# A planner of on-chip buffers: a half buffer passes over a just-freed half when more than three slots are free, not more than seven

## The chip, the cores and the metric

The kernel runs on one core of a Trainium2 chip. The metric is the device time of one execution in microseconds. "Before" is the kernel as it was, "after" the kernel with the change. A step is one count of the kernel's `self.i`, mostly one product of 24 matmuls.

## The reference

One inference step of a small decoder of two layers, a pooling mixer (layer A) and an attention mixer (layer B), for 1024 prompt tokens and 8 sample tokens, model width 2048, all in float32.

```python
def pool_layer(x, prefix, pos, w_in, w_grp, scale, w_out, g_ln, b_ln):
    z = x @ w_in                                   # 2048 x 4096
    u, gate = z[..., :D_POOL], z[..., D_POOL:]
    d, new_state = multiscale_pool(u, prefix, pos) # trailing means over 2, 4, 8, 16
    d = einsum('btgc,gce->btge', d in 4 groups, w_grp) * scale
    y = (d * silu(gate)) @ w_out
    return layer_norm(ALPHA * x + y, g_ln, b_ln), new_state

def attn_layer(x, pos, kb, vb, ..., w_in, sinks, w_out, g_ln, b_ln):
    z = x @ w_in                                   # queries and gate
    q = rope_partial(z[..., :D_ATTN], pos)
    o = attn_core(q, kb, vb, q_pos, k_pos, sinks)  # window of 128, 4 KV heads, a sink per head
    y = (o * silu(gate)) @ w_out
    return layer_norm(ALPHA * x + y, g_ln, b_ln)
```

Between the two, keys and values are projected once (`w_kv`). The outputs are both token sets and the new pooling states, keys and values.

## The kernel before

The tokens are cut into two chunks: chunk 0 has 512 prompt tokens, chunk 1 the other 512 and the 8 sample tokens. The work runs in phases: `ai` (the input projection of layer A) for chunk 0 and 1, `ao` (its output projection), `bi` (keys, values, queries, gates and attention of layer B) and `bo` (its output projection). The names below carry the chunk: `bi1`, `bo0`.

Nearly all products are done by a Strassen-like scheme (`seven`): seven products of 1024 x 128 weights with half a chunk of tokens instead of eight, their results added and subtracted by ScalarE (ACT) and VectorE (DVE) while TensorE (PE) goes on. float32 values are split into a high and a low part of the type fp32r (`cast_to` by ACT, L508; `prep_to` by DVE, L523), and each product takes three matmuls for each of eight blocks (L687, L688, L689): 24 matmuls. The sums of weight blocks that the scheme needs are made on DVE (L352 in `first_pair`, `sum_gen` at L460 and above) and stored to DRAM by POOL for the other chunk.

The order of the work is fixed when the program is built. PE, DVE and ACT each carry out their instructions in the order of the source (`in_order`); SP issues nearly all loads and POOL nearly all stores, each in its own order. What falls to one step is settled by the planner: `begin` loads, casts and prepares weights some products ahead, `end` runs what was put down for the step (`product`, `at`), the token blocks of the next phase (`x_tick`) and side work (`sum_gen`, `t_gen`, `ln_gen`). Several of these ask how many slots are whole: `begin` looks less far ahead with under three (`bi1`) or five (`bo0`) whole slots, `sum_gen` of `wob` starts a load only with more than five, `x_tick` and the side work have bounds of their own.

All working buffers come from one pool, `Mem`: 54 slots, each of two halves. `full` takes the whole free slot that was given back longest ago. `half` takes the free half of a slot whose other half is in use ("part-free"), the one given back longest ago, or else half of a whole free slot. Time is counted by `clock`, one tick for each buffer given back. A buffer that a store still reads is given back with `free(True)` and counts as ten ticks younger. Who writes a buffer next must wait until its last readers are done: the planner's choice decides whom a writer waits for.

Lines that matter below:

- L626 to L658: the steps of `seven`. `p2` (L631, L632) takes a half, `o["s"]`, and ACT copies a PSUM bank into it; `p4` (L653) is DVE's last reading, after which it is freed. L635, L641, L647, L660 are ACT's other copies out of a bank.
- L925 to L939: `j_steps`, the sum of a pair of rows for a mean: `add` takes a half and DVE writes the sum (L929), ACT casts it (L935), DVE takes the rest (L939) and frees the half. `j_sum` is the matmul behind it (L955).
- L1374: `shifted` puts these three at steps n, n+1, n+2 in `bo0` for its first pair; L1344 is the residual sum ahead of it, L1383 and L1387 use the mean.
- L1753 to L1770: `rope` takes a half that a load fills (L1755), and gives it back to a store.
- L1961, L1962, L1977: the softmax weights leave PSUM (ACT, DVE), and PE multiplies them with the values.
- L1984 to L1989: `gate` takes a half, DVE writes the attention's result (L1986), POOL stores it (`o<-m`, L1989), and the half is given back with `free(True)`.
- L2040: `decode`, the attention of the sample tokens, a chain of ten short steps through all engines: L2096 to L2098 are DVE's part of the softmax, L2102 PE's transpose behind it, L2105 the copy of that. Its second half runs at the start of `bo0`.

Of the kernel before, what the change touches and what calls it, by code (L numbers as in the profile page):

```python
# [139 lines left out]
class Mem:  # L140
# [22 lines left out]
    def half(self, n=TMAX):  # L163
        fits = lambda i: i < NWIDE or n <= 512
        part = [
            (a if b is None else b, i) for i, (a, b) in enumerate(self.f) if (a is None) != (b is None) and fits(i)
        ]
        if part and min(part)[0] > self.clock - 6 and len(self.whole()) > 7:
            part = []
        i = min(part)[1] if part else min((i for i in self.whole() if fits(i)), key=lambda i: max(self.f[i]))  # L170
        h = 0 if self.f[i][0] is not None else 1
        if not part:
            self.new(i)
        self.f[i][h] = None
        w = TMAX if i < NWIDE else 512
        return Slot(self, i, h, self.t[i][:, h * w : (h + 1) * w])
# [2332 lines left out]
```

## Time and profile before

| | |
|---|---|
| median of 3 runs | 2312.7 us (2311.48 to 2317.13) |
| profiled execution | 2315.52 us, its span 2313.7 us |
| PE busy | 2285.5 us, 99% of the span |
| DVE, ACT, POOL busy | 1904.7, 1388.2, 218.4 us |
| mean granted clock of PE | 0.997 |
| DMA | 647.77 MB, mean 280 GB/s |

How to read it. The busy time of PE is the union of its matmuls, which overlap: one lasts some 282 ns, and the next starts long before its end. A wait is put down as "who, line <- whom it waited for"; in a row of the time order the wait stands in brackets behind the instruction that waited. The span's time axis places the phases: `bi0` begins at about 1075 us, `bi1` at about 1500, `bo0` at about 1940, `bo1` at about 2125.

### The profile page before, as it was taken

Reading aid. Unit: us, or ns where it says so; the run is one execution under the profiler, and the core shown is the slowest. Engines: PE = TensorE matmul, PEld = TensorE weight load, DVE = VectorE, ACT = ScalarE, POOL = GpSimd, SP = SyncE. Lnnn points to the kernel's source line nnn. Section 1 sums busy time; section 2 is a strip of 40 time slices with the busy share of each in tenths; the row PEclk is TensorE's granted clock in tenths of the full one; section 3 lists DMA queues with packets and bytes.
Section 4 is the critical chain, followed back from the end, with each engine's and each line's share of the span. In section 5 each row is a group of like instructions: output and inputs, shape, how many; then the busy total and the mean of one; then the engine's idle time right before and its main releaser. Section 6 shows DMA issues by size and latency. Waiting matters only on the chain. (4 is left out here: it accounts for less than half of the span.)

```text
span 2313.7 us, 50523 instructions
## 1 busy us (share of the span) xinstructions
PE 2285.5 (99%) x20353; PEld 2214.5 (96%) x20353; DVE 1904.7 (82%) x2413; ACT 1388.2 (60%) x2551; POOL 218.4 (9%) x399
## 2 busy tenths in 40 slices
PE   9999999999999999999999999999999999899998
PEld 8999999999999999999889999999999999899998
DVE  8888889877878878988868888899776777788997
ACT  5544446444546556555567676785676678556665
POOL 0111110010000000000111111100010100010001
PEclk9999999999999999999999999999999999999999
DMA  7779679988889989999777767777776779699894
GB/s 259 266 263 316 228 249 330 314 305 301 301 305 322 338 286 331 320 385 343 236 249 238 243 225 251 268 264 234 242 247 224 250 238 315 210 359 363 297 333 150
DMA packets 252028, 647.77 MB, mean 280 GB/s; under 512 B 27504, under 2 KB 112528, under 8 KB 251792
## 3 DMA queue, kind: packets, MB, share of 16 engines
q1 hardware_dynamic: 208640, 490.20, 63.2%
q0 software_dynamic: 43152, 154.34, 17.3%
q8 instruction: 159, 2.61, 0.5%
q14 instruction: 77, 0.63, 0.1%
HBM read 467.21 MB, written 177.23 MB: 279 GB/s over the span
## 5 line engine op out<-in xcount | busy, mean ns | idle before, releaser
L687 PE MATMUL pD<-m,m 128*128 128x260 f32 (+1 forms) x5088 | 1443.6, 284 | 4.9 <-ACT pD L626 2.2
L689 PE MATMUL pD<-m,m 128*128 128x260 f32 (+1 forms) x5088 | 1436.2, 282 | 6.0 <-DVE m L523 5.7
L688 PE MATMUL pD<-m,m 128*128 128x260 f32 (+1 forms) x5088 | 1436.5, 282 | 0.0
L687 PEld LDWEIGHTS pD<-m,m 128*128 128x128 f32 x5088 | 960.7, 189 | 14.8 <-issue 7.2
L689 PEld LDWEIGHTS pD<-m,m 128*128 128x128 f32 x5088 | 961.4, 189 | 8.0 <-DVE m L523 8.0
L688 PEld LDWEIGHTS pD<-m,m 128*128 128x128 f32 x5088 | 960.8, 189 | 0.5
L523 DVE TENSOR_TENSOR m<-m,m 128x1024 fp32r<-128x1024 f32 x690 | 833.4, 1218 | 94.6 <-ACT m L508 32.2
L508 ACT CAST m<-m 128x1024 fp32r<-128x1024 f32 x690 | 720.6, 1049 | 231.6 <-DVE m L352 118.5
L352 DVE TENSOR_TENSOR m<-m,m 128x1024 f32<-128x1024 f32 x136 | 166.2, 1222 | 15.1 <-DMA m<-in_wia 10.4
L850 DVE TENSOR_TENSOR m<-m,m 128x1024 fp32r<-128x1024 f32 (+1 forms) x118 | 144.0, 1225 | 4.4 <-ACT m L841 3.8
L841 ACT CAST m<-m 128x1024 fp32r<-128x1024 f32 (+1 forms) x118 | 123.4, 1053 | 4.5 <-DMA m<-in_x 2.4
L648 DVE TENSOR_TENSOR m<-pD,m 128x260 f32<-128x260 f32 (+1 forms) x92 | 39.0, 424 | 101.4 <-ACT pD L647 95.3
L660 ACT COPY m<-pD 128x260 f32<-128x260 f32 (+1 forms) x88 | 32.8, 372 | 122.4 <-PE pD L689 121.8
L1935 ACT ACTIVATE m<-m,sm 128x128 f32<-128x128 f32 x256 | 99.3, 392 | 0.0
L632 ACT COPY m<-pD 128x260 f32<-128x260 f32 (+1 forms) x90 | 33.6, 373 | 97.8 <-PE pD L689 93.1
L1184 PE MATMUL pD<-m,m 128*128 128x260 f32 (+1 forms) x528 | 91.5, 323 | 0.0
L715 PE MATMUL pD<-m,m 128*128 128x512 f32 x224 | 89.0, 397 | 0.0
L635 ACT COPY m<-pD 128x260 f32<-128x260 f32 (+1 forms) x92 | 34.4, 374 | 90.8 <-PE pD L689 90.7
L717 PE MATMUL pD<-m,m 128*128 128x512 f32 x224 | 88.2, 394 | 0.0
L716 PE MATMUL pD<-m,m 128*128 128x512 f32 x224 | 88.2, 394 | 0.0
L1184 PEld LDWEIGHTS pD<-m,m 128*128 128x128 f32 x528 | 79.4, 188 | 8.2
L1948 ACT ACTIVATE m<-m,sm 128x128 f32<-128x128 f32 x256 | 81.9, 393 | 2.7 <-DVE sm L1943 2.5
(259 smaller groups left out, 2082.4 us busy)
## 6 DMA issues: line engine op xcount, KB each, us to landing
m<-in_wib SPq DMA_DIRECT2D x132, 512.0 KB
m<-in_wia SPq DMA_DIRECT2D x128, 512.0 KB
m<-swoa SPq DMA_DIRECT2D x64, 512.0 KB
swia<-m POOLq DMA_DIRECT2D x56, 512.0 KB, 4.6
m<-swia SPq DMA_DIRECT2D x56, 512.0 KB
m<-swob SPq DMA_DIRECT2D x56, 512.0 KB
m<-in_wob SPq DMA_DIRECT2D x52, 512.0 KB
m<-in_woa SPq DMA_DIRECT2D x48, 512.0 KB
```

What stands on the lines that cost most here:

```text
L352: self.nc.vector.tensor_add(s[out].a[:, :1024], s[x].a[:, :1024], s[y].a[:, :1024])
L508: self.nc.scalar.copy(hi.r[:, :1024], self.stream[self.cast].src().a[:, :1024])
L523: self.nc.vector.tensor_sub(lo.r[:, :1024], s.src().a[:, :1024], hi.a[:, :1024])
L687: nc.tensor.matmul(ps[:, :TH], wh[:, s], h, start=new and k == 0, stop=False, skip_group_check=on)
L688: nc.tensor.matmul(ps[:, :TH], wh[:, s], l, start=False, stop=False, skip_group_check=on)
L689: nc.tensor.matmul(ps[:, :TH], wl[:, s], h, start=False, stop=k == 7, skip_group_check=on)
L715: nc.tensor.matmul(ps[:], wh[:, s], h, start=par == 0 and k == 0, stop=False)
L716: nc.tensor.matmul(ps[:], wh[:, s], l, start=False, stop=False)
L841: self.nc.scalar.copy(h.r[:, :n], s.a[:, :n])
L850: self.nc.vector.tensor_sub(l.r[:, :n], s.a[:, :n], h.a[:, :n])
L1184: nc.tensor.matmul(ps[:, : cs.stop - cs.start], ws[:, s], d[:, cs], start=f0 and k == 0, stop=l0 and k == 3,)
L1935: nc.scalar.activation(x["s3"][:, i, :], x["s3"][:, i, :], AF.Exp, bias=nm[:, i : i + 1], scale=0.125, accum_out=rs[:, i : i + 1],)
```

## The change

In `Mem.half`, a part-free half that was given back within the last six ticks is passed over, and a whole free slot is opened instead, when more than three slots are whole. Before, that took more than seven. Everything else is the same code.

```diff
-        if part and min(part)[0] > self.clock - 6 and len(self.whole()) > 7:
+        if part and min(part)[0] > self.clock - 6 and len(self.whole()) > 3:
             part = []
```

The slots of all later buffers can differ from the first request on at which the two conditions differ, and with them the number of whole slots that the planner's other bounds read.

## The prediction

> **What bounds the kernel now.** I read the page's head first, then the busy time by stretch, then who waited for whom in the stretch where TensorE lost most, then DVE, PE and POOL in order of time there.
>
> ```profile
> span 2313.7 us, 50523 instructions
> PE 2285.5 (99%) x20353; PEld 2214.5 (96%) x20353; DVE 1904.7 (82%) x2413; ACT 1388.2 (60%) x2551; POOL 218.4 (9%) x399
> ```
> ```profile
> core 0: us, PE busy (x) PEld busy (x) DVE busy (x) ACT busy (x) POOL busy (x), PEclk, DMA share, GB/s
> 700.00:900.00 200.00, 200.00 (x1689) 199.92 (x1688) 160.03 (x185) 114.76 (x162) 10.72 (x18) 1.00 0.90 312
> 1232.00:1500.00 268.00, 267.86 (x2988) 261.43 (x2987) 230.18 (x279) 186.15 (x445) 43.80 (x84) 1.00 0.71 244
> 1560.00:1990.00 430.00, 428.45 (x4719) 417.96 (x4719) 322.11 (x444) 295.36 (x690) 37.00 (x58) 1.00 0.75 246
> 1990.00:2060.00 70.00, 63.33 (x549) 62.17 (x548) 58.05 (x74) 35.05 (x58) 8.01 (x15) 0.95 0.81 286
> 2000.00:2010.00 10.00, 6.00 (x41) 5.87 (x43) 7.57 (x10) 3.23 (x5) 0.53 (x1) 0.66 0.29 101
> 2060.00:2100.00 40.00, 37.77 (x308) 37.57 (x307) 32.84 (x45) 19.32 (x27) 3.73 (x7) 0.96 1.02 391
> ```
>
> PE is the bound: it idles 28.2 us of the span (2313.7 - 2285.5), so a change that leaves the matmuls alone can win only there and in the granted clock. In bi0 and bi1 (1232 to 1990) PE idles 0.14 us of 268 and 1.55 us of 430. The one place with a real hole is the start of bo0, 1990 to 2060: 6.7 us idle, and the clock at 0.95.
>
> ```profile
> PE pS L2102 <- DVE m L2098: 5.3, 1, 5.3
> DVE m L929 <- DMA o<-m: 4.9, 1, 4.9
> ACT m L1383 <- PE pO L955: 3.3, 1, 3.3
> DVE m L2105 <- PE pS L1977: 3.1, 1, 3.1
> ACT m L632 <- DVE m L939: 2.6, 1, 2.6
> ```
> ```profile
> 1994.27 1.22 DVE L523 TENSOR_TENSOR m<-m,m 128x1024 fp32r<-128x1024 f32 x1
> 2000.39 0.69 DVE L929 TENSOR_TENSOR m<-m 128x512 f32<-128x512 f32 x1 [4.91 <-DMA o<-m]
> ...
> 2003.66 0.29 DVE L2098 TENSOR_SCALAR m<-m,sm 128x128 f32<-128x128 f32 x1
> ...
> 2006.26 1.22 DVE L1962 TENSOR_TENSOR m<-pS,cst 128x1024 f32<-128x1024 f32 x1
> 2007.39 0.68 DVE L939 TENSOR_TENSOR m<-m,m 128x512 fp32r<-128x512 f32 x1
> 2011.18 0.29 DVE L2105 COPY m<-pS 128x128 f32<-128x128 f32 x1 [3.11 <-PE pS L1977]
> ```
> ```profile
> 1992.75 0.54 POOL L1989 DMA_DIRECT2D o<-m  x1 [0.29 <-issue]
> ```
> ```profile
> DMA to landing us min/median/max: 7.6/7.6/7.6
> ```
> ```profile
> 2004.00 0.47 PE L2102 MATMUL pS<-cst,m 128*128 128x128 f32 x1 [5.28 <-DVE m L2098]
> 2004.13 0.56 PE L687 MATMUL pD<-m,m 128*128 128x256 f32 x1
> ...
> 2008.54 0.34 PE L689 MATMUL pD<-m,m 128*128 128x256 f32 x1
> 2008.72 0.28 PE L687 MATMUL pD<-m,m 128*128 128x256 f32 x1
> ...
> 2009.16 1.53 PE L1977 MATMUL pS<-m,m 128*64 128x128 f32 x24
> ```
>
> The reader is to see a chain. `gate` stores its half by POOL at 1992.75, and that store lands 7.6 us later, at 2000.3. The sum of L929 (`j_steps`, the first step of `shifted`) is to be written into the very half that the store reads, because the allocator handed it out one step after it was given back. DVE works in order, so L929 holds it for 4.91 us, and the short operations of `decode` behind it (L2096 to L2098) come late; PE's transpose L2102 waits 5.28 us for them. The clock then falls: 0.66 over 2000 to 2010.
>
> **The change part by part.** It adds and removes no instruction. It lets `half` pass over a part-free slot given back in the last six ticks when 4 to 7 slots are whole; before, that took 8. I wrote out the slot list of the kernel before, step by step (a step is one count of `self.i`). Of its 182 requests for a half, 14 meet the new condition and not the old: bi0 steps 404, 432, 446, 460; bi1 523, 537, 551, 558, 564, 593; bo0 625 and 628; bo1 703 and 708. Up to step 404 nothing can differ. Between those steps the slots in use differ for four or five steps and then agree again in number, since the extra slot is whole once its half is freed.
>
> *Step 625, bo0, is L929.* Five slots are whole, the half is seven ticks short of its due age (a stored half is put back ten ticks into the future). The new rule takes the oldest whole slot, which held weights of the product of step 624. PE stands at steps 626 and 627 by then, so nothing is left to wait for, and L929 starts when the L523 before it ends, 1994.27 + 1.22 = 1995.49, not 2000.39: 4.90 us earlier. From the start of L929 to the end of L2098 DVE takes 2003.66 + 0.29 - 2000.39 = 3.56 us, all its own work; L2098 ends at 1999.05 and PE goes on at 1999.10 in place of 2004.00. An idle time of 0.4 us stays (5.28 - 4.90).
>
> The clock: from 2004.13 to 2008.72, 22 matmuls (L687 to L689 in turn; the first and the last rows are shown) took 4.59 us. At the pace of the stretch 700 to 900, 200 us for 1689, they take 22 x 0.118 = 2.61 us. With 0.4 us of idle time left I expect no fall of the clock, so 1.98 us more are won.
>
> What is late next: the products of L1977 need what L1962 writes. PE would reach L1977 at 1999.10 + 0.13 + 2.61 + (2009.16 - 2008.72) = 2002.28. L1962 ends at 2007.48 before, 2002.58 after. PE waits 0.3 us there. So L1977 starts at 2002.58 for 2009.16: **6.6 us** (4.9 + 2.0 - 0.3). Right behind, DVE waits for PE (L2105, 3.1) and ACT too (L1383, 3.3), so both are tied to PE again and the rest shifts as a whole.
>
> I set the clock's part by the row and not by a rule. [...]
>
> *Step 628, bo0,* is the copy of L632 that waited 2.6 us for L939 (the same half, just freed). It takes a slot that PE has read. ACT gains 2.6 us, PE nothing I can see: that copy's bank is next written three products later, 3 x 24 x 0.118 = 8.5 us. If it all passed to PE, 2.6 more are won.
>
> *The ten in bi0 and bi1.* Waits of this kind in the trace of before (SP's own waits, then the line L632, then ACT's waits from 1200 us on):
>
> ```profile
> SPq L1755 <- DMA o<-m: 7.3, 1, 7.3
> ```
> ```profile
>   DMA o<-m: 1.7, 1
> ```
> ```profile
> ACT m L508 <- DVE m L523: 25.0, 19, 3.3
> ```
>
> The first, at `take` of step 564, holds SP's queue and the weight loads behind it for 7.3 us; the second is the copy of L632 at step 558, on ACT. Both should go, and both count nothing: PE idles only 1.55 us in all of 1560 to 1990, so loads and copies there already come early enough (the prepared weights cover them; without it, 7.3 at most). The other eight pass over a half that nobody still reads for a whole slot that is often younger (at 432, 446 and 460 two ticks against four). In bi0 that slot held weights of the very product whose result the copy reads, so no new wait. In bi1 two could wait for DVE's L523, in the third row 3.3 us at the longest for ACT; the 8.5 us of slack cover it. I take 0, with -3.3 and +1.7 us as ends. The two of bo1 (703, 708) are copies of L632 as well: 0.
>
> The profiled execution took 2315.5 us with a span of 2313.7; the median of the three runs is 2312.7, 2.8 less. The sum of 6.6 makes 2308.9 of the one and **2306.1** of the other.
>
> **The rivals.**
>
> *The second hole goes too, or another is opened.*
>
> ```profile
> DVE m L898 <- DMA m<-o: 2.4, 1, 2.4
> PE pD L689 <- DVE m L523: 2.2, 1, 2.2
> ```
> ```profile
> o<-m POOLq DMA_DIRECT2D x32, 256.0 KB, 5.4
> ```
>
> At 2090 a load came late and DVE's L898 held L523, with a PE stall of 2.2 us and a clock of 0.96 over 40 us (1.6 us): 3.8 us. The load waits for a slot; with the slots dealt anew it may come earlier: 2306.1 - 3.8 = 2302.3. Against it: the order of requests by age is the same, only the slots' numbers differ. The same numbers put a floor under the main case: stores of this kind land in 5.4 us in the median, 2.2 less than this one. In a run where it does so, the wait is 2.7, the gain 4.4, the time 2308.3.
>
> *The whole lowered stretch counts.* If the falling clock costs (1 - 0.66) x 10 = 3.4 us and not 2.0, the time is 2304.7. The 2.2 us of the stretch before 2004.00, when PE had nothing to do, speak against it. [...]
>
> *The wait stays.* The rule needs more than three whole slots at step 625. There are five; if the earlier changes leave two more in use, the half is taken again and the time is 2312.7, give or take 2. For it: the sums of `wob` start only with more than five whole slots, so in bi1 they slip by some steps. Against it: from step 606 to 616 between 10 and 26 are whole, room enough to catch up, and the loads of bo0 are forced by due times.
>
> *Slower: the look-ahead is cut in bi1.* `begin` prepares fewer weights ahead with under three whole slots. Before, at steps 546, 547, 560, 563 and 567 exactly three are whole; one more in use cuts there. If each cut ended as at 2090, 3.8 us, two would bring 2313.7, no gain at all, and all five 2312.7 - 6.6 + 19.0 = 2325.1; from two on it is slower than before, from four on clearly. Against it: at 502 and 556 two whole slots did cut it, and PE idled for neither by more than the 1.55 us of its stretch. [...]
>
> **How the numbers follow.** About 0.3%, 6.9 us, is what a measurement of this kernel can tell from no change: 2305.8 and 2319.6. Main case 0.58, own range 2303.5 (6.6 + 2.6 won) to 2308.5; the second hole 0.12; the whole stretch 0.05; the wait stays 0.17; slower 0.08. Faster: 0.12 + 0.05 and 0.22 of the main case, which lies astride the bound: 0.39. Slower by over 0.3%: most of the last, 0.07. The rest, 0.54, is no change that can be told. The range goes from 2302 to 2314, with the second hole and the wait that stays inside, and leaves out the cuts.
>
> **What would show it.** Right: no DVE L929 waiting for o<-m, PE's wait before L2102 under 1 us, a clock near 1.00 in the 20 us behind it, L1977 some 6.6 us earlier against the start of bo0, ACT's L632 without its 2.6 us, and SP's L1755 without its 7.3. Wrong: L929 or another DVE operation behind a store, a new PE stall of over 2 us with the clock down, or PE idle in bi0 and bi1 above its 1.7 us.

## The result: 2305.7 us, and the profile after

| | before | after |
|---|---|---|
| median of 7 runs each | 2313.93 us (2311.48 to 2317.13) | 2305.71 us (2303.34 to 2309.14) |
| ratio, 95% interval | | 0.9967 [0.9955, 0.9978] |
| profiled execution's span | 2313.7 us | 2303.9 us |

The change wins 8.2 us, 0.33%; 2306.1 was predicted. The head of the page and the busy time by stretch of the kernel after (columns as before: busy time and instructions of each engine, granted clock, DMA share, GB/s):

```profile
span 2303.9 us, 50527 instructions
PE 2281.2 (99%) x20353; PEld 2211.1 (96%) x20353; DVE 1905.1 (83%) x2413; ACT 1387.5 (60%) x2551; POOL 217.7 (9%) x399
```
```profile
1232.00:1500.00 268.00, 267.90 (x2989) 261.46 (x2988) 230.80 (x281) 185.37 (x446) 43.83 (x84) 1.00 0.70 244
1560.00:1990.00 430.00, 428.46 (x4725) 418.24 (x4723) 323.85 (x445) 297.81 (x695) 37.58 (x59) 1.00 0.74 246
1990.00:2060.00 70.00, 68.51 (x610) 67.48 (x611) 62.14 (x78) 37.11 (x59) 7.48 (x14) 1.00 0.90 328
2060.00:2100.00 40.00, 38.09 (x322) 37.89 (x322) 32.35 (x45) 20.56 (x29) 3.73 (x7) 1.00 1.02 389
```

The busy instructions of each engine are as many as before. In bi0 and bi1 (the first two rows) PE idles what it idled before, 0.1 and 1.5 us. At the start of bo0 it idles 1.5 us of 70 in place of 6.7, and the clock is at 1.00 in place of 0.95. The same place in order of time, first DVE, then PE:

```profile
1992.88 1.22 DVE L523 TENSOR_TENSOR m<-m,m 128x1024 fp32r<-128x1024 f32 x1
1994.02 0.69 DVE L929 TENSOR_TENSOR m<-m 128x512 f32<-128x512 f32 x1
...
1997.28 0.29 DVE L2098 TENSOR_SCALAR m<-m,sm 128x128 f32<-128x128 f32 x1
...
1999.88 1.22 DVE L1962 TENSOR_TENSOR m<-pS,cst 128x1024 f32<-128x1024 f32 x1
2001.01 0.68 DVE L939 TENSOR_TENSOR m<-m,m 128x512 fp32r<-128x512 f32 x1
2003.16 0.29 DVE L2105 COPY m<-pS 128x128 f32<-128x128 f32 x1 [1.47 <-PE pS L1977]
```
```profile
1997.62 0.33 PE L2102 MATMUL pS<-cst,m 128*128 128x128 f32 x1 [0.58 <-DVE m L2098]
2001.15 1.97 PE L1977 MATMUL pS<-m,m 128*64 128x128 f32 x32 [0.36 <-DVE m L1962]
```

L929 no longer carries a bracket: it starts as soon as the L523 ahead of it lets it. PE's wait before L2102 is 0.58 us (5.28 before), and the next wait is the one the prediction named, 0.36 us for L1962. From the moment PE runs out of work ahead of L2102 to the start of L1977, 10.44 us passed before (2009.16 - 2004.00 + 5.28) and 4.11 after (2001.15 - 1997.62 + 0.58): 6.3 us won here.

The spans differ by 9.8 us. Some 1.9 of the other 3.5 lie at the second hole. Waits of the kernel after from 2060 to 2100:

```profile
DVE m L898 <- DMA m<-o: 2.2, 1, 2.2
PE pD L689 <- DVE m L523: 1.9, 1, 1.9
```

The hole is still there, 1.9 us for 2.2, but the clock behind it stayed at 1.00 (0.96 over the 40 us before, some 1.6 us by (1 - 0.96) x 40). The last 1.6 us were already there at 1990; the medians of the experiments show nothing of that size from the steps before it.

### The profile page after: what moved, and what is told of

Its sections match the earlier page's. It is cut to its first block, busy times and chain, and to the rows that moved or that the text cites. A ratio compares the mean times of both kernels' runs of the same rounds, so it can differ in the third digit from the quotient of the medians.

```text
span 2303.9 us, 50527 instructions
## 1 busy us (share of the span) xinstructions
PE 2281.2 (99%) x20353; PEld 2211.1 (96%) x20353; DVE 1905.1 (83%) x2413; ACT 1387.5 (60%) x2551; POOL 217.7 (9%) x399
## 5 line engine op out<-in xcount | busy, mean ns | idle before, releaser
L523 DVE TENSOR_TENSOR m<-m,m 128x1024 fp32r<-128x1024 f32 x690 | 833.0, 1217 | 92.3 <-ACT m L508 38.6
L1935 ACT ACTIVATE m<-m,sm 128x128 f32<-128x128 f32 x256 | 99.3, 391 | 0.0
L632 ACT COPY m<-pD 128x260 f32<-128x260 f32 (+1 forms) x90 | 33.6, 373 | 93.5 <-PE pD L689 93.2
L626 ACT ACTIVATE pD<-pD 128x260 f32<-128x260 f32 (+1 forms) x90 | 33.2, 369 | 83.6 <-PE pD L689 83.0
```

Source lines behind the costliest of these rows:

```text
L523: self.nc.vector.tensor_sub(lo.r[:, :1024], s.src().a[:, :1024], hi.a[:, :1024])
L1935: nc.scalar.activation(x["s3"][:, i, :], x["s3"][:, i, :], AF.Exp, bias=nm[:, i : i + 1], scale=0.125, accum_out=rs[:, i : i + 1],)
```

## The experiments

Eight kernels, in two groups of four; each group was timed against the kernel before on the same chip (medians 2312.74 and 2312.83 us). Inserted lines move the numbers of what follows by one to three in some of them: L930 is L929, L2103 is L2102, and so on.

**Step 625 alone.**

```diff
-        if part and min(part)[0] > self.clock - 6 and len(self.whole()) > 7:
+        if part and min(part)[0] > self.clock - 6 and len(self.whole()) > (3 if self.kern.i == 625 else 7):
```

(`self.kern` is the kernel, which `Mem` is given for this.)

> The kernel before with the new bound of three at step 625 alone; all other requests keep seven. Theory A (the one wait of L929 for the store o<-m, with the clock behind it): 6.3 us less than before (a staircase of 4.7 us at L2102 and 2.0 us of clock behind it, less 0.4 us at L1977), and no DVE wait of L929 in the trace; the wait of L632 for L939 (2.6 us) goes or stays without a mark on the time. Rival B (the gain is spread over the other changed requests): at most 2 us less than before, the wait of PE before L2102 turns up elsewhere.

2306.38 us, ratio 0.9973 [0.9963, 0.9983]: 6.4 us won by one decision. PE's and DVE's waits from 1980 to 2012, whole (those of the weight loads left out):

```profile
DVE m L2078 <- PE pS L2072: 4.4, 1, 4.4
...
DVE m L2106 <- PE pS L1978: 1.5, 1, 1.5
...
PE pD L688 <- ACT m L661: 1.1, 1, 1.1
DVE m L1388 <- ACT m L1384: 1.0, 1, 1.0
...
PE pS L1978 <- DVE m L1963: 0.4, 1, 0.4
...
PE pS L2103 <- DVE m L2099: 0.3, 1, 0.3
```

No DVE instruction waits for a store there, and nothing took the place of PE's wait. This is theory A's outcome. Its profiled execution, with 2308.95 us the longest of the eight, lost clock at the second hole, as before:

```profile
PE pD L690 <- DVE m L524: 2.5, 1, 2.5
```
```profile
2060.00:2100.00 40.00, 37.51 (x305) 37.31 (x304) 31.93 (x45) 19.51 (x27) 3.73 (x7) 0.96 1.00 382
```

**All but step 625.** The same line with 7 and 3 exchanged.

> The new bound of three everywhere but at step 625, where seven stays. Theory A: L929 waits some 5 us for the store again, PE before L2102 as well, the clock falls behind it, and the time is that of before, within 1.5 us. Rival B: most of the gain of the change is there, 5 us or more less than before.

2313.11 us, ratio 0.9999 [0.9991, 1.0008]. The chain is back:

```profile
PE pS L2103 <- DVE m L2099: 5.4, 1, 5.4
DVE m L930 <- DMA o<-m: 4.7, 1, 4.7
```

Eleven other requests followed the new rule here and won nothing. Rival B falls.

**A bound of four, and of five.** `> 4` and `> 5` in the same line.

> The bound is four in place of three. At step 625 five slots are whole, so the half is passed over; at steps 565 and 628 four are whole, so there the half is taken as before. Theory A: the time of the change with three, within 1.5 us (6 to 8 us less than before), though ACT's L632 waits 2 to 3 us for L939 again. Rival (the freed ACT at step 628 is part of the gain): up to 2.6 us of the gain is lost.

> The bound is five. At step 625 five are whole, which is not more than five, so the half is taken there as before; steps 404, 537 and 593, with six whole, follow the new rule. Theory A: the time of before within 1.5 us, with L929's wait of about 5 us in the trace. Rival B (the other requests matter): 2 us or more less than before.

With four 2304.77 us, 0.9968 [0.9956, 0.9980], the gain of the change; with five 2311.89, 0.9996 [0.9987, 1.0005], none. At step 625 five slots are whole, and the time goes by which side of five the bound lies. Waits of the kernel with five at that place:

```profile
PE pS L2102 <- DVE m L2098: 5.0, 1, 5.0
DVE m L929 <- DMA o<-m: 4.4, 1, 4.4
ACT m L632 <- DVE m L939: 2.7, 1, 2.7
```

With four, I expected ACT's wait of 2 to 3 us for L939 at step 628 to come back. It did not, and the expectation was careless: once the sum of step 625 lies in another slot, the part-free half at step 628 is the one that `gate`'s store has left, not the one of L939. ACT's copy ran at 1997.73 there, ahead of L939 at 1999.85. Step 628's wait was a consequence of step 625's, and its own decision is worth nothing.

**A delay of DVE put back by hand.** The changed kernel, in which the sum of L929 is made nine times, or five, at step 625:

```diff
-            self.nc.vector.tensor_add(box["u"].a[:, :T], a, b)
+            for _ in range(9 if self.i == 625 else 1):
+                self.nc.vector.tensor_add(box["u"].a[:, :T], a, b)
```

> The changed kernel, in which DVE makes the sum of L929 at step 625 nine times in place of once (the same sum into the same half), so some 4.8 us of DVE work stand where the wait for the store stood. Theory A (what counts is how late DVE is at this place, whatever makes it late): PE waits some 5.4 us before L2102, the clock falls behind it, and 5 to 6.5 us of the gain go: 2311 to 2312. Rival B (the gain lies in other slots or transfers): PE does not wait there as long, and less than 2 us go.

> The changed kernel with five sums in place of one, 2.4 us of DVE work. Theory A: PE waits some 3.0 us before L2102. If the clock holds, 2.0 us of the gain go (2307.8); if it falls as in the kernel before, up to 4 us (2309.7). This tells what a wait of 3 us costs in clock at this place.

Nine sums: 2312.73 us, 1.0001 [0.9991, 1.0010] of before, so the whole gain is gone with the slots of the changed kernel all in place. The time lies above the 2311 to 2312 that was expected, since more was put back than the store had held: the nine took 6.49 us (0.72 each; I had reckoned with 0.60), 5.8 more than the one sum, against the store's 4.9. PE waited longer than foreseen, and the clock fell:

```profile
1993.35 6.49 DVE L930 TENSOR_TENSOR m<-m 128x512 f32<-128x512 f32 x9
```
```profile
PE pS L2103 <- DVE m L2099: 6.4, 1, 6.4
```
```profile
2000.00:2010.00 10.00, 7.24 (x57) 6.97 (x57) 6.73 (x9) 3.02 (x5) 0.53 (x1) 0.66 0.52 170
```

Five sums: 2309.93 us, 0.9987 [0.9978, 0.9996], just past the upper end of what was expected; 2.9 us under before are left. Its L2102 and L1977, and the clock:

```profile
2000.58 0.48 PE L2103 MATMUL pS<-cst,m 128*128 128x128 f32 x1 [3.45 <-DVE m L2099]
...
2005.12 1.09 PE L1978 MATMUL pS<-m,m 128*64 128x128 f32 x16
```
```profile
2000.00:2010.00 10.00, 9.43 (x80) 9.04 (x81) 6.42 (x9) 3.51 (x6) 0.53 (x1) 0.83 0.72 244
```

The wait grew by 2.87 us (3.45 - 0.58), and from PE running out of work to L1977 there are 7.99 us (2005.12 - 2000.58 + 3.45), 3.9 more than in the changed kernel. The 0.36 us of wait for L1962 fell away, so 1.4 us are the clock's (3.88 - 2.87 + 0.36); the clock's row alone gives an estimate of (1 - 0.83) x 10 = 1.7. So the waits at this place, 3.45 us here and 5.28 before, cost themselves and 1.4 to 2 us of clock.

**The transpose one step later, in the kernel before.**

```diff
-DEC_AT = (3, 4, 6, 6, 7, 8, 9, 10, 13, 13), (11, 11, 12, 12, 13, 14, 15, 16, 17, 17)
+DEC_AT = (3, 4, 6, 6, 7, 8, 9, 10, 13, 13), (11, 11, 12, 12, 13, 14, 16, 16, 17, 17)
```

> The kernel before with the transpose of decode's softmax (L2102) put down for step 628 in place of 627, so PE has one product more to do ahead of it. Theory A (DVE's order is the cause: L1962 stands behind L929 too): PE waits for L1962 ahead of L1977 instead, some 4 to 6 us, and the time is that of before within 2 us. Rival D (the late chain of decode alone is the cause): PE waits no longer than 2.5 us, and 4 us or more are won.

2311.85 us, 0.9997 [0.9988, 1.0006]: no gain. PE does not wait at L2102 any more, and waits elsewhere:

```profile
ACT m L935 <- DVE m L929: 5.0, 1, 5.0
DVE m L929 <- DMA o<-m: 4.5, 1, 4.5
...
PE pD L687 <- ACT pD L626: 2.9, 1, 2.9
...
PE pD L689 <- DVE m L523: 0.8, 1, 0.8
```

This is theory A's time, by a way that I had not named. What came late first was not L1962 but ACT: its L935 waits for L929 and holds back L626, the step of `seven` that opens the next product's bank (L935 starts at 1999.82, L626 at 2000.35, the product at 2000.77). Two engines in order stood behind the store, so taking the short chain of `decode` out of PE's way opens the next wait.

**Loads two ahead at the second hole.** The changed kernel, in `t_gen`:

```diff
+        n = 2 if key[0] == "o" else 1
+        if n == 2:
+            load(1)
...
-            if kp < 7:
-                load(kp + 1)
+            if kp + n < 8:
+                load(kp + n)
```

> The changed kernel with the loads of t_gen for the tokens o of chunk 1 two pairs ahead in place of one, for the second hole (DVE's L898 waits 2.2 us for m<-o, PE behind it 1.9 us). If that wait is what holds PE there: 1.9 us less than the changed kernel, and none of the runs loses clock there, 2303 to 2304. Rival: the load waits for a slot or for the other transfers and comes as late as before; no change.

2304.91 us, 0.9967 [0.9954, 0.9980]: against the changed kernel's 2305.71 (2303.34 to 2309.14) no difference that these runs can tell. The wait of L898 is gone and PE is busy throughout the stretch, but waits for L523 turn up after it. The stretch, and PE's wait from 2100 to 2140:

```profile
2060.00:2100.00 40.00, 40.00 (x340) 40.00 (x339) 32.16 (x45) 20.48 (x29) 3.73 (x7) 1.00 1.00 363
```
```profile
PE pD L689 <- DVE m L523: 1.8, 3, 0.9
```

So the 2303 to 2304 us that were expected did not come: of the 1.9 us won, 1.6 were given back within the next 40. In those 40 us DVE is busy without a break, 40.00 us here and in the changed kernel, so PE waits there for DVE to get through its own work, not for a load. The three waits of at most 0.9 us cost no clock that the runs show: the mean granted clock of all five was 0.999, and their times lay between 2303.99 and 2306.17.

## Why the prediction was right

*The place and the chain.* The argument rested on one row, L929 waiting 4.91 us for `o<-m`. Step 625 alone wins 6.4 us; everything else together is 0.4 us slower by its median, which is nothing.

*The sum.* L929 and L2098 early: PE's wait fell by 4.7 us (4.9 predicted). The new wait for L1962: 0.36 (0.3). With 6.3 us won up to L1977, 6.33 - 4.70 + 0.36 leave 2.0 us for the clock, as taken from the 22 matmuls. The term in total is 6.3 for 6.6. Charging the whole lowered stretch of before, (1 - 0.66) x 10 = 3.4 us, does not agree with the trace: PE had no work in the first 2.17 of its 6.83 us, and the loss was 2.0. In the kernel with five sums, where PE works through nearly the whole of its lowered stretch (busy for 9.43 of the 10 us from 2000), the same estimate, 1.7 us, comes close to the 1.4 measured.

*Step 628 and the ten of bi0 and bi1 at nothing.* Right in the time. Of the two waits that were to go there, the copy of L632 lost its wait for a store, as the other copy lost the one for L939. All that ACT's idle time before L632 waits for in the kernel after:

```profile
  PE pD L689: 93.2, 67
```

The one of SP's queue only moved to another load, as SP's waits from 1700 to 1800 in the kernel after show:

```profile
SPq L288 <- DMA o<-m: 7.2, 1, 7.2
...
SPq L1755 <- DVE sm L2096: 4.2, 1, 4.2
```

PE covered the one as it had covered the other. Neither came about in the way that the prediction gave: in the slot list of the kernel after, no part-free half is there to be passed over at steps 558 and 564, because the requests before them had dealt the slots anew. Two more steps of bi1, 560 and 567, have under three whole slots and a shorter look-ahead. The prediction's last rival had priced such a cut at 3.8 us; these left no mark, with 1.5 us of idle time in 1560 to 1990, before and after.

*The second hole.* I held it to stay, and it did; that the clock behind it held in the profiled execution is 1.6 us that no step of the sum had. The kernel with step 625 alone lost them in its profile and gains 6.4; the one with a bound of four kept them and gains 8.0. That fits the way from 6.6 us to 8.2, but the intervals of these ratios overlap, so it is not shown. Executions of one kernel differ in it, too: of the seven of the changed kernel, the four with a mean granted clock of 0.999 took 2303.3 to 2305.7 us, the three with 0.997 and 0.998 took 2307.3 to 2309.1. (At which place these three lost clock is not on record.)

*How near the number came.* Some of that is luck. The gain was 1.6 us larger than the sum, and the median of before was 1.2 us higher than that of the three runs from which the sum set out (2313.93 and 2312.7); the two nearly cancel in 2306.1 and 2305.7.

*The wait stays.* It needed fewer than four whole slots at step 625. In the slot list of the kernel after there are again five, and twelve requests between steps 404 and 703 pass over a half that the old bound would have handed out, eleven of them at steps that I had listed (the twelfth is at 565).

## What to carry to other kernels

In a kernel whose busiest engine is at 99%, look for the one wait that stands alone: here 4.9 us of a store in one decision of an allocator were all of the effect that the runs can tell, of a rule that touched a dozen. Price such a wait at the engine that sets the end, with the next wait behind it (0.36 us here) and the clock that the pause costs (2.0 us here, behind a wait of 5.28), and check on which side of the new bound that one decision falls. A buffer that a store still reads is a costly one to hand to an engine that works in order: here the store landed 7.6 us after its issue, DVE's L929 waited 4.91 us for it, and all that stood behind that writer waited too, on DVE and on PE, which it feeds (5.28 us).

## What the runs showed of the hardware

In the trace of the kernel before, the granted clock is 0.50 from 2001.83 to 2008.66 (6.83 us) and from 2093.99 to 2097.40 (3.41 us), each time behind a wait of PE, and 1.00 around them; it is 0.50 once more from 2309.03 on, when PE's matmuls are done. In the trace of the kernel after it is below 1.00 only past 2300, behind the last matmul. The start of bo0 before, cut where the clock changes and where PE goes on:

```profile
1990.00:2001.83 11.83, 7.65 (x64) 7.24 (x62) 6.75 (x12) 6.40 (x18) 1.61 (x3) 1.00 0.83 289
2001.83:2004.00 2.17, 0.00 (x0) 0.00 (x0) 2.10 (x6) 1.14 (x2) 0.00 (x0) 0.50 0.03 11
2004.00:2008.66 4.66, 4.66 (x22) 4.66 (x23) 4.04 (x4) 1.38 (x2) 0.53 (x1) 0.50 0.18 72
2008.66:2060.00 51.34, 51.02 (x465) 50.27 (x464) 45.16 (x54) 26.13 (x37) 5.87 (x11) 1.00 0.90 316
```

The lowered stretch begins while PE still waits: 2.17 us of it pass without a matmul. The 22 matmuls behind take 4.66 us, 0.21 each for 0.118 at a clock of 1.00. With five sums they start 0.21 us apart in the lowered stretch, too (2001.06 to 2003.62), and 0.12 apart behind it. At the second hole before, the clock fell at 2093.99, when PE had been back at work since 2092.63; PE was busy in all 3.41 us of that stretch.

Here are PE's longest wait and the clock at both places, in one profiled execution of each kernel:

| | longest wait, 1980 to 2012, us | clock, 1990 to 2060 | wait at the second hole, us | clock, 2060 to 2100 |
|---|---|---|---|---|
| before | 5.3 | 0.95 | 2.2 | 0.96 |
| after | 0.8 | 1.00 | 1.9 | 1.00 |
| step 625 alone | 1.1 | 1.00 | 2.5 | 0.96 |
| all but step 625 | 5.4 | 0.95 | 1.5 | 1.00 |
| bound of four | 0.8 | 1.00 | 1.5 | 1.00 |
| bound of five | 5.0 | 0.98 | 1.6 | 1.00 |
| nine sums | 6.4 | 0.95 | 1.5 | 1.00 |
| five sums | 3.5 | 0.98 | 2.0 | 0.96 |
| transpose later | 2.9 | 0.98 | 2.6 | 0.96 |
| loads two ahead | 0.8 | 1.00 | none | 1.00 |

In these executions the clock lost was not in proportion to the wait: with 5.0 us (bound of five) the clock was 0.98, with 5.3 (before) 0.95, an estimated 1.4 us and 3.5 by (1 - clock) x 70; with 2.9 us (transpose later) it was 0.98 as with 5.0. At the second hole it stayed at 1.00 with 1.9 us (after) and fell to 0.96 with 2.0 (five sums), an estimated 1.6 us by (1 - 0.96) x 40. What decides between these was not shown. Between the profiled executions of before and after, the hole itself differs by 0.3 us and the clock behind it by those 1.6.
